# An interleaved HGRN2 and Conformer trunk: VectorE and ScalarE of the first stage in written order, the recurrence's output in the keys' tile, the seam by hand

## The chip, the core and the metric

The kernel runs on one core of a Trainium2 chip. A core has five engines that run their own instruction streams in order: TensorE (PE in the profile) for matrix products, VectorE (DVE), ScalarE (ACT), GpSimd (POOL) and SyncE (SP), which here only issues transfers. They meet through semaphores. An instruction whose semaphore has not come holds up everything behind it on its engine. Products go to PSUM, in eight banks of 128 x 512 floats; everything else lives in SBUF. The metric is the device time of one execution in microseconds (us); lower is better. All values are 32-bit floats.

## The reference, cut to what matters

Two layers over a sequence of 1024 tokens with 1024 channels. The change touches the mixer of the first layer:

```python
def hgrn2_mixer(h, w_in, lb, norm_g, w_out):
    q, fz, v, g = jnp.split(h @ w_in, 4, axis=-1)
    q = silu(q)
    f = lb + (1 - lb) * sigmoid(fz)          # the forget gate
    k = 1 - f
    # per head (8 heads, 128 keys, 128 values), along the tokens:
    #   S_t = diag(f_t) S_{t-1} + k_t v_t^T ,   o_t = S_t^T q_t
    o = recurrence(q, k, v, f)
    o = o * rsqrt(mean(o * o, axis=-1) + RMS_EPS) * norm_g
    return (o * silu(g)) @ w_out
```

What follows (the layer norm, two squared-ReLU networks, a Conformer convolution module as the second mixer, two more layer norms) is the same in both kernels.

## The kernel before

The first stage computes the four projections, the recurrence and the start of the product with w_out. A pair is two blocks of 128 output channels, computed for both halves of the tokens (512 each) with seven products in place of eight (Strassen's scheme, in Winograd's form): `PAIRS` lists twelve pairs, eight of kind q (one head's queries and forget gates) and four of kind g (two heads' output gates), and `ORDER` the seven products, numbered 1, 2, 6, 5, 7, 3, 4. Each product is four quarter products of three matmuls, because each operand is kept as a rounded high part and a low part. `make_form` prepares the weight operand of a product: sums on DVE (tiles pr, total), the high part by a cast on ACT, the low part by a subtraction on DVE (tile fs, in a ring of five). `load_block` fetches the next weight block on SP when a block is used up.

`pair_product` issues a product; after it, its result is taken out of PSUM into a tile t, added to others, and passed through the gate functions by `settled` and `swish` (tiles sq, qk, t). The results of kind q go to the tile qk (queries and keys of one head, 128 x 2048), those of kind g wait in one of four tiles t.

`recurrence(h)` is a generator: each `yield` ends a step. In order: the forget gates F and first scalings; scalings of the queries and keys by products of gates over 1, 2, 4, ... 64 tokens (`scale`, `total`, on DVE, tiles qk and T); between them PE's level products (`levels`), whose results DVE copies under a mask into the tile at (`put`); the transposes of the keys, which ACT copies to the tile kt; the states, a chain of small DVE operations on PE's outer products (`outer`); the outputs (`attend`); the statistics (`settle`: squares on ACT, a scaling on DVE, a power on POOL, copies on ACT to the tile F, called o); and the transposes back (`give`), whose result ACT writes to the tile F again (called on) and SP stores to DRAM (od). Two heads run at a time, the second at least nine steps (`LAG`) behind the first. F, T, kt, kd and at exist once.

`slot()` runs after each quarter product. It counts a tick, which starts jobs that `later` has put off, and by `pace` it lets `step()` take one step of a recurrence. So the order on PE, POOL and SP is the written one, in which the recurrence's steps stand between quarter products. The order on DVE and ACT in this stage is not: after `early_order.close()` a scheduler with a timeline model chooses it. `gate_some` and `gate_out` load a stored head half (u), multiply it with its gate, and store it (zd).

`block_sums` adds weight blocks of the later networks in DRAM: two plain copies of 1 MB on SP, then three accumulating transfers on POOL. Twelve of them fall into this stage.

The last pair overlaps with the loading and splitting of w_out (tiles wb, wa) and of the gated heads (tile back to oT) in `tail`; then the first three output blocks of w_out are computed with seven of eight row blocks each, the last head is finished (`last_head`), and the eighth row block follows.

In the profile most DVE, PE and POOL instructions have line 173, the helper that issues them. They are told apart by their tiles.

Of the kernel before, what the change touches and what calls it, by code (L numbers as in the profile page):

```python
# [15 lines left out]
P = 128  # L16
# [3 lines left out]
H = 8  # L20
# [217 lines left out]
def body(ctx, tc, d, out):  # L238
# [102 lines left out]
    order.enter_context(tc.manual_schedule(engines={mybir.EngineType.PE, mybir.EngineType.Pool, mybir.EngineType.SP}))  # L341
# [106 lines left out]
    early_order = ExitStack()  # L448
    early_order.enter_context(tc.manual_schedule(engines={mybir.EngineType.DVE, mybir.EngineType.Activation}))
# [99 lines left out]
    def make_form():  # L549
# [5 lines left out]
        hi, lo = s[:, 0], s[:, 1]  # L555

        def plus(out, x, y):
            vector.tensor_tensor(out=out, in0=x, in1=y, op=ALU.add)

        if i == 6:  # L560
# [5 lines left out]
        if i == 2:  # L566
            plus(b[0], b[0], b[2])
        made.append(s)
        if i in (5, 7, 3, 4):
            free.append(b[{5: 2, 7: 0, 3: 1, 4: 3}[i]])  # L570
            load_block()
# [16 lines left out]
    def recurrence(h):  # L588
# [3 lines left out]
        F = p1("f")  # L592
        vector.tensor_scalar(out=F, in0=K, scalar1=GATE_EPS, scalar2=None, op0=ALU.max)
        nc.scalar.activation(K, K, AF.Identity, bias=qs, scale=-QSCALE)
        mul(Q, Q, F)
        T = p1("T")
# [15 lines left out]
        def grow(n):  # L612
            total(n)
            scale(n)

        def levels(a, b, n=P):
            for s in range(0, n2, n):
                tensor.matmul(level_ps[:, s // P, :], a[:, s : s + n], b[:, s : s + n], start=True, stop=True)
# [3 lines left out]

        total(1)
        yield
        scale(1)
        yield
        grow(2)
# [9 lines left out]
        scale(4)  # L637
        yield
# [11 lines left out]
        scale(16)  # L650
        total(32)
        yield
        for n in (32, 64):
# [3 lines left out]
            scale(n)  # L657
            if n == 32:
                total(64)
# [9 lines left out]
        nc.scalar.copy(out=kt[:, :nk], in_=level_ps[:, :nk])  # L669
        yield  # L670
        state = None
        o, on = F.rearrange("p (a b) -> p a b", b=P), F

        def settle(half):
            ss = stat.tile([P, 2, 4], F32, tag="ss", name="ss")
            sq = p1("sq")
            for c in range(NTB):
                nc.scalar.activation(sq[:, c * P : (c + 1) * P], out_ps[:, half * NTB + c, :], AF.Square, scale=1.0 / QSCALE, accum_out=ss[:, 0, c : c + 1])
            vector.tensor_scalar(out=ss[:, 1], in0=ss[:, 0], scalar1=1.0 / P, scalar2=RMS_EPS, op0=ALU.mult, op1=ALU.add)
            power_m_half(ss[:, 0], ss[:, 1], 4)  # L680
            for c in range(NTB):
                nc.scalar.activation(o[:, half * NTB + c], out_ps[:, half * NTB + c, :], AF.Copy, scale=ss[:, 0, c : c + 1])

        def give(half):
            part = slice(half * HT, (half + 1) * HT)
            for c in range(half * NTB, half * NTB + NTB):
                tensor.transpose(out_ps[:, c, :], o[:, c], ident)
            nc.scalar.activation(on[:, part], out_ps[:, half * NTB : half * NTB + NTB].rearrange("p a b -> p (a b)"), AF.Copy, scale=nrm[:, h : h + 1])
            if h == H - 1:
# [56 lines left out]
    def settled(kind, j, m, n, t, ps=None):  # L746
        if kind == "g":
            if t is None:
                t = p1("t")
# [887 lines left out]
```

## Time and profile before

| | us |
|---|---|
| median of three runs (lowest, highest) | 2174.51 (2171.23, 2177.52) |
| the profiled execution | 2174.34 |
| its span, on which all positions below are counted | 2172.5 |
| PE, DVE, ACT, POOL busy in it | 2103.5, 1451.1, 1043.4, 369.0 |

The pair products start at 91.3 us and the stage's last waits of PE lie before 504 us. The views used below are: the busy times of the engines, in the whole and in stretches (PE, weight load, DVE, ACT and POOL, then the mean granted clock of PE, the DMA share and GB/s); the list of waits (who waited for whom: total us, times, longest us); the chain that ended last (start, us, what); groups of instructions (busy us and mean ns of one, then the idle time before them); instructions in order of time, with the idle time before them in brackets; and the transfers by their issuing queue (KB, median us from issue to landing). PEld is the weight load of PE, which overlaps its products.

### The profile page before, as it was taken

To read this page: it belongs to the slowest core of one execution; us is meant where nothing else is said; L and a number is where in the kernel's file an instruction comes from. 1 tells how busy PE (TensorE), PEld (TensorE's weight loads), DVE (VectorE), ACT (ScalarE), POOL (GpSimd) and SP (SyncE) were. 2 spreads that over 40 slices of the span, in tenths; PEclk is the share of its full clock that TensorE was granted. 3 is DMA by queue.
4 is the path that set the end of the run, shared out by engine and by line. 5 is a ranking of instruction groups with operands and counts; after the bars stand their busy time and mean duration, and the time that the engine had idled before them with its cause. 6 is when DMAs were issued, how large, how long until landed. Compare 5 with 4: busy or idle time off the path is not lost.

```text
span 2172.5 us, 27149 instructions
## 1 busy us (share of the span) xinstructions
PE 2103.5 (97%) x10056; PEld 1747.4 (80%) x10056; DVE 1451.1 (67%) x1890; ACT 1043.4 (48%) x1599; POOL 369.0 (17%) x344
## 2 busy tenths in 40 slices
PE   8998897899999999999999999999999999999998
PEld 6777786777888888888888888888878888888886
DVE  8596776776777666656666799799727544554446
ACT  5444343343156555644445576558542443443333
POOL 0011111100100000000001499289211000000001
PEclk9999999999999999999999999999999999999999
DMA  4486887755269976899998855664495888866552
GB/s 177 164 228 169 236 210 198 186 141 207 79 192 300 306 277 213 285 387 326 342 332 319 301 193 179 219 241 166 158 312 206 316 323 308 313 203 194 194 165 98
DMA packets 174357, 508.62 MB, mean 234 GB/s; under 512 B 16528, under 2 KB 45456, under 8 KB 173200
## 3 DMA queue, kind: packets, MB, share of 16 engines
q1 hardware_dynamic: 165264, 473.32, 61.3%
q0 software_dynamic: 8960, 33.56, 8.7%
q8 instruction: 79, 1.29, 0.2%
q14 instruction: 54, 0.44, 0.1%
HBM read 377.32 MB, written 196.61 MB: 264 GB/s over the span
## 4 chain that ended last, share of the span: by engine, by line
PE 82%; DMA 6%; DVE 6%; POOL 3%; issue 1%; ACT 1%; SPq 0%; DVEq 0%; POOLq 0%; ACTq 0%
PE ps L173 82%; POOL cb L173 3%; DMA od<-f 2%; DVE qk L173 1%; DMA wa<-ready 1%; DMA raw<-in_w_dram 1%; DMA u<-od 1%; DMA pr<-in_wp_dram 1%; DMA vr<-in_wv_dram 1%; DVE at L173 0%; DVE vr L173 0%; DVE fs L173 0%; DVE xf L173 0%; DVE t L173 0%; ACT xf L390 0%
## 5 line engine op out<-in xcount | busy, mean ns | idle before, releaser
L173 PE MATMUL ps<-dw,dh 128*128 128x512 f32 x2688 | 611.0, 389 | 0.0
L173 PEld LDWEIGHTS ps<-dw,dh 128*128 128x128 f32 x2688 | 504.3, 188 | 104.3
L173 PE MATMUL ps<-x1f,fw 128*128 128x512 f32 x1344 | 307.9, 390 | 0.8 <-DVE c L173 0.8
L173 PEld LDWEIGHTS ps<-x1f,fw 128*128 128x128 f32 x1344 | 251.5, 188 | 52.9 <-issue 1.2
L173 PE MATMUL ps<-xa,wa 128*128 128x512 f32 x1152 | 268.8, 392 | 0.0
L173 PE MATMUL ps<-xf,fs 128*128 128x512 f32 x1008 | 264.2, 413 | 0.0
L173 PEld LDWEIGHTS ps<-xa,wa 128*128 128x128 f32 x1152 | 214.3, 188 | 43.3
L173 POOL TENSOR_TENSOR cb<-cb,prod 128x512 f32<-128x512 f32 x176 | 234.3, 1341 | 17.6 <-ACT prod L1405 7.1
L173 PEld LDWEIGHTS ps<-xf,fs 128*128 128x128 f32 x1008 | 192.3, 198 | 38.6
L173 DVE TENSOR_TENSOR dh<-dh 128x1024 fp32r<-128x1024 f32 x112 | 136.5, 1223 | 114.1 <-ACT dh L70 114.0
L173 DVE TENSOR_TENSOR dw<-dr,dw 128x1024 fp32r<-128x1024 f32 x112 | 136.7, 1223 | 105.3 <-ACT dw L70 104.8
L173 DVE SCALAR_TENSOR_TENSOR ps<-u,par,ps 128x512 f32<-128x512 f32 x288 | 198.7, 750 | 9.9 <-ACT ps L1417 8.5
L70 ACT CAST dh<-dh 128x1024 fp32r<-128x1024 f32 x112 | 117.1, 1050 | 144.9 <-DMA dh<-hf 143.0
L70 ACT CAST dw<-dr 128x1024 fp32r<-128x1024 f32 x112 | 117.4, 1053 | 138.7 <-PE ps L173 126.4
L173 PE MATMUL ps<-xc,wa 128*128 128x512 f32 x768 | 174.4, 389 | 0.0
L173 PEld LDWEIGHTS ps<-xc,wa 128*128 128x128 f32 x768 | 144.1, 188 | 29.8
L475 POOL TENSOR_TENSOR mv<-mv,nhalf 128x1 f32<-128x1 f32 x32 | 46.3, 1447 | 681.3 <-DVE mv L173 681.3
L1405 ACT ACTIVATE prod<-u,par 128x512 f32<-128x512 f32 x176 | 125.3, 722 | 54.1 <-POOL cb L173 53.3
L173 DVE TENSOR_TENSOR wa<-raw,wa 128x1024 fp32r<-128x1024 f32 x55 | 71.4, 1300 | 69.6 <-ACT wa L70 69.5
L70 ACT CAST wa<-raw 128x1024 fp32r<-128x1024 f32 x55 | 57.8, 1050 | 118.4 <-PE ps L173 108.8
L173 PE MATMUL ps<-vw,xf 128*128 128x512 f32 x336 | 82.1, 408 | 9.2 <-ACT vw L390 5.1
L173 PE MATMUL ps<-xb,wa 128*128 128x512 f32 x384 | 89.3, 391 | 0.0
(196 smaller groups left out, 2609.5 us busy)
## 6 DMA issues: line engine op xcount, KB each, us to landing
wa<-ready SPq DMA_DIRECT2D x122, 512.0 KB, 4.6
dh<-hf SPq DMA_DIRECT2D x112, 512.0 KB, 4.8
ready<-spare SPq DMA_DIRECT2D x74, 512.0 KB, 4.8
sum_w<-in_w_dram SPq DMA_DIRECT2D x32, 1024.0 KB, 9.4
dr<-sum_w SPq DMA_DIRECT2D x64, 512.0 KB, 4.4
raw<-in_w_dram SPq DMA_DIRECT2D x51, 512.0 KB, 4.4
dr<-in_w_dram SPq DMA_DIRECT2D x48, 512.0 KB, 4.6
raw<-in_w1q_dram SPq DMA_DIRECT2D x36, 512.0 KB, 4.3
```

The lines of the kernel that those rows point to most:

```text
L70: self.nc.scalar.copy(out=slot[:, 0, c], in_=raw[:, c])
L173: return op(*args, **kw)
L475: nc.gpsimd.tensor_tensor(out=dst, in0=src, in1=nhalf[:, :n], op=ALU.pow)
L1405: nc.scalar.activation(tp, u[:, k : k + HT], AF.Copy, scale=tap(j, k))
```

## The change

1. DVE and ACT follow the written order through the whole first stage. For that the operations that depend on PE or on one another are put off with `later`: a product's result is taken out one quarter product after its end (`evacuate`), a gate's multiplication two after its sigmoid, the low part of a weight form one after the high part, each scaling and masked copy of the recurrence one after the products it follows, the copies after the statistics three after the squares. One form more is made ahead, and a head joins the waiting recurrences four quarter products later.
2. The normalised output is written into kt (`on`), not F; the squares go to F, not to sq; the statistics' scaling runs on POOL, not on DVE.
3. The loads of u, the multiplications with the gates and the stores are paced by ticks (`gate_turn`): a load at least seven ticks after the head's store, the product at least nine after the load, the store two after it. The product is written over the gate, and that tile is stored.
4. The two plain copies of `block_sums` in this stage are issued by POOL.
5. The end of the stage is a list of jobs with ticks (`seam`): loads and splits of w_out and of the heads, two heads to an operation. The first three output blocks are computed together, row block by row block.

```diff
-    order.enter_context(tc.manual_schedule(engines={mybir.EngineType.PE, mybir.EngineType.Pool, mybir.EngineType.SP}))
+    order.enter_context(tc.manual_schedule(engines={getattr(mybir.EngineType, e) for e in ("PE", "Pool", "SP", "DVE", "Activation")}))
...
+        queue = nc.sync if after is not None else nc.gpsimd
...
-        nc.sync.dma_start(out=v[:, 0:2], in_=w[:, 0:4:2])
-        later(gap // 2, lambda: nc.sync.dma_start(out=v[:, 2:4], in_=w[:, 0:2]))
+        queue.dma_start(out=v[:, 0:2], in_=w[:, 0:4:2])
+        later(gap // 2, lambda: queue.dma_start(out=v[:, 2:4], in_=w[:, 0:2]))
...
-        cut(hi, lo, total if i == 6 else b[{1: 0, 2: 1, 5: 2, 7: 0, 3: 1, 4: 3}[i]])
...
+        def low():
+            vector.tensor_tensor(out=lo, in0=raw, in1=hi.bitcast(F32), op=ALU.subtract)
+            if i == 2:
+                plus(b[0], b[0], b[2])
+            if i in (5, 7, 3, 4):
+                free.append(raw)
+                load_block()
+        def high():
+            nc.scalar.copy(out=hi, in_=raw)
+            later(wait, low)
+        later(wait if i in (6, 5) else 0, high)
...
         levels(K, Q)
-        grow(8)
-        put(1)
+        total(16)
+        later(1, lambda: (scale(8), put(1)))
         yield
         levels(kd[:, 1], kd[:, 0])
-        put(0)
-        total(16)
+        total(32)
+        later(1, lambda: put(0))
         yield
...
-        put(2)
         dec = p1("dec")
-        vector.tensor_copy(out=dec, in_=totals[P])
+        later(1, lambda: (scale(64), put(2), vector.tensor_copy(out=dec, in_=totals[P])))
         yield
...
-        o, on = F.rearrange("p (a b) -> p a b", b=P), F
+        o, on = F.rearrange("p (a b) -> p a b", b=P), kt.rearrange("p a b -> p (a b)")
...
-            for c in range(NTB):
-                nc.scalar.activation(sq[:, c * P : (c + 1) * P], out_ps[:, half * NTB + c, :], AF.Square, scale=1.0 / QSCALE, accum_out=ss[:, 0, c : c + 1])
-            vector.tensor_scalar(out=ss[:, 1], in0=ss[:, 0], scalar1=1.0 / P, scalar2=RMS_EPS, op0=ALU.mult, op1=ALU.add)
+            for c in cs:
+                nc.scalar.activation(o[:, c], out_ps[:, c, :], AF.Square, scale=1.0 / QSCALE, accum_out=ss[:, 0, c % NTB : c % NTB + 1])
+            nc.gpsimd.tensor_scalar(out=ss[:, 1], in0=ss[:, 0], scalar1=1.0 / P, scalar2=RMS_EPS, op0=ALU.mult, op1=ALU.add)
             power_m_half(ss[:, 0], ss[:, 1], 4)
+            def rest():
+                for c in cs:
+                    nc.scalar.activation(o[:, c], out_ps[:, c, :], AF.Copy, scale=ss[:, 0, c % NTB : c % NTB + 1])
+                ready.add(half)
+            later(3, rest)
...
         outer(range(NTB))
+        later(1, lambda: chain(range(NTB)))
         yield
         attend(range(NTB))
         outer(range(NTB, nk))
-        settle(0)
+        later(1, lambda: (chain(range(NTB, nk)), settle(0)))
...
+            if k == 3:
+                later(1, lambda: evacuate(p, i, st, ps))
+            slot()
...
+    def gate_turn():
+        now = ticks[0]
+        if to_load and len(loaded) < 2 and done.get(to_load[0], now) <= now - 7:
+            at = to_load.pop(0)
+            u = p1("u")
+            nc.sync.dma_start(out=u, in_=od[at[0]][at[1]])
+            loaded.append((at, u, now))
+        if loaded and loaded[0][0] in gates and loaded[0][2] <= now - 9:
+            (h, half), u, _ = loaded.pop(0)
+            g = gates.pop((h, half))
+            mul(g, u, g)
+            def store():
+                nc.sync.dma_start(out=zd[half][:, h, :], in_=g)
+                stored[h, half] = ticks[0]
+            later(2, store)
...
+    def seam():
+        plan = [
+            (5, lambda: fetch(0, 0)), (15, lambda: split_w(0, 0, 136)), (17, lambda: split_w(0, 1, 144)), (19, lambda: split_w(0, 3, 120)),
+            (21, lambda: split_w(0, 2, 152)), (13, lambda: heads_in(0, 0, 4, 32)), (19, lambda: heads_in(0, 4, 6, 32)),
...
+            (43, lambda: last_in(H - 2, 1, sixth[1])), (46, lambda: last_in(H - 1, 1, lastly[1])),
+        ]
+        for n, job in plan:
+            later(n, job)
...
+    make_form()
+    tick(4)
...
         if kind == "q":
-            recs.append(j)
+            later(4, lambda j=j: recs.append(j))
...
+    for k in range(KB):
+        for (t, n), ps in zip(early_out, (banks[:, i] for i in range(3))):
+            (lh, ll), (rh, rl) = wide(oT[0][0], t, ws[n])[k]
+            tensor.matmul(ps, lh, rh, start=k == 0, stop=False)
+            tensor.matmul(ps, lh, rl, start=False, stop=False)
+            tensor.matmul(ps, ll, rh, start=False, stop=k == KB - 1)
             slot()
```

More of the change, by code (lines that the diff above doesn't have):

```diff
@@ L626, in recurrence @@
         yield
-        grow(2)
+        total(2)
+        scale(2)
         yield
@@ L695, in recurrence @@
[L695 to L697 removed]
+                done[h, half] = ticks[0]
+            later(1, end)
         def values(c):
@@ new lines, in body, with take, silu, evacuate @@
+    recs, active, pace, alone = [], [], [0.0, 0.0], [False]
+    LAG = 9
+    def take():
+        at = owners["at"] % 4
+        owners["at"] += 1
+        assert owners.get(at) not in gates, owners[at]
+        owners[at] = None
+        return p1("t"), at
+    owners = {"at": 0}
+    def silu(out, t, then):
+        sg = p1("sq")
+        nc.scalar.activation(sg, t, AF.Sigmoid)
+        later(2, lambda: (mul(out, t, sg), then()))
+    def evacuate(p, i, st, ps):
+        kind, j = PAIRS[p]
+        m, n = {2: (0, 0), 7: (1, 1), 3: (0, 1)}.get(i, (1, 0))
+        def gate(t, at):
+            def then():
+                gates[2 * j + m, n] = t
+                owners[at] = (2 * j + m, n)
+            return then
+        if i in (1, 6, 5):
+            st[i] = take()
+            nc.scalar.copy(out=st[i][0], in_=ps)
@@ L766, in body @@
+        if kind == "g":
+            later(1, lambda: silu(t, t, gate(t, at)))
+        elif m == 0:
+            later(1, lambda: silu(qk[j][:, 0, part], t, lambda: None))
+        else:
+            later(1, lambda: gated_key(t, 1.0))
     turn_of = {"z": 0, "a": 1, "b": 2}
     def pair_product(p, i, f, st):
-        kind, j = PAIRS[p]
         ps = banks[:, st["banks"]["a" if i == 2 else "b" if i in (5, 3) else "z"]]
```

263 lines of the change are left out of this document (96 added, 167 removed).

## The prediction

> **What bounds the kernel now.** I read the page, then the busy time by stage, the waits of the stage that the change touches, and its chain.
>
> ```profile
> PE 2103.5 (97%) x10056; PEld 1747.4 (80%) x10056; DVE 1451.1 (67%) x1890; ACT 1043.4 (48%) x1599; POOL 369.0 (17%) x344
> PE 82%; DMA 6%; DVE 6%; POOL 3%; issue 1%; ACT 1%; SPq 0%; DVEq 0%; POOLq 0%; ACTq 0%
> ```
> ```profile
> 91.30:504.00 412.70, 365.17 (x2244) 309.04 (x2243) 302.21 (x464) 183.26 (x419) 50.31 (x51) 0.95 0.75 201
> 620.00:1400.00 780.00, 779.17 (x3519) 646.09 (x3518) 550.48 (x695) 440.47 (x608) 167.00 (x171) 1.00 0.80 281
> 1400.00:2172.00 772.00, 761.02 (x3409) 629.16 (x3407) 447.98 (x519) 344.88 (x458) 137.11 (x104) 0.99 0.66 229
> ```
>
> TensorE bounds the whole, and from 620 us on it is idle for 12 us in all. In the 412.7 us of the pair products and the recurrence (the busy times stand in the order PE, weight load, DVE, ACT, POOL, then the clock) it is idle for 412.7 - 365.2 = 47.5 us, and its granted clock is 0.95 on average. DVE is the next busiest, 302 us or 73%. Who holds PE up, and who holds up DVE:
>
> ```profile
> PE ps L173 <- DVE qk L173: 25.7, 11, 6.0
> PE ps L173 <- DVE at L173: 18.2, 7, 5.5
> DVE ss L173 <- ACT sq L678: 16.9, 13, 3.3
> DVE u L173 <- DMA u<-od: 11.8, 6, 5.9
> DVE total L173 <- DMA pr<-in_wp_dram: 9.5, 3, 5.6
> DVE f L173 <- DMA od<-f: 9.2, 4, 4.4
> ```
> ```profile
> 172.70 9.65 DMA od<-f
> ...
> 182.45 0.71 DVE f L173
> ...
> 183.18 1.23 DVE qk L173
> ...
> 188.27 1.80 PE ps L173 x33
> ```
> ```profile
> 188.27 1.07 PE L173 MATMUL ps<-qk 128*32 128x32 f32 x32 [5.95 <-DVE qk L173]
> 227.83 2.46 PE L173 MATMUL ps<-kd 128*128 128x128 f32 x12 [4.36 <-DVE at L173]
> 286.47 1.07 PE L173 MATMUL ps<-qk 128*32 128x32 f32 x32 [3.59 <-DVE qk L173]
> 377.08 3.78 PE L173 MATMUL ps<-qk 128*128 128x128 f32 x16 [5.53 <-DVE at L173]
> ```
>
> Nearly all PE idle time is a level product of the recurrence that waits for DVE's scaling (qk) or its masked copy (at). The chain shows why: a store of the finished head out of tile F lands after 9.65 us, DVE stands at the next head's first write to F, and the older head's scaling is queued behind it. Of the four gaps, 188 and 286 are of this kind; 227 comes after DVE's wait for u, 377 after its wait for weights.
>
> The stops also cost clock:
>
> ```profile
> 138.00:144.00 6.00, 3.61 (x39) 2.98 (x38) 6.00 (x8) 1.56 (x2) 1.12 (x3) 1.00 0.72 171
> 186.00:192.00 6.00, 3.73 (x38) 3.10 (x39) 6.00 (x9) 1.23 (x2) 0.00 (x0) 0.62 0.91 251
> 192.00:198.00 6.00, 6.00 (x34) 4.67 (x33) 6.00 (x8) 1.54 (x3) 0.00 (x0) 0.81 0.00 0
> ```
>
> After 2.4 us of idle (138 to 144) it stays 1.00; after the gap of 5.95 us it is 0.62, and then 0.81 with PE fully busy. At most 0.05 x 365 = 18 us are lost so in the stage; I take 15, since the dips stand where PE works. So 47.5 + 15 = 62.5 us can be had here, no more.
>
> **The change part by part.** (1) The output goes into the keys' tile: the 9.2 us of DVE waits go. The store must now land before the same tile takes the next head's keys. In the written order that write stands more than ten quarter products behind the second store, over 7 us by the row of a product below, with the recurrence's own products between; a landing of 9.65 us, as above, about fits. The squares now go to F as well, which nothing else uses at that time. I count nothing; the bounds are 0 and the 9.65 us, once a head, if every store were late.
>
> (2) DVE and ACT in written order, each operation one to three quarter products behind its source. PE keeps its work; only the recurrence's steps move, by up to four quarter products. The gate load is issued nine quarter products ahead of its product, so the 11.8 us of u go; the 16.9 us of ss move to POOL. What is late next is DVE itself, in arrears where a written stretch asks more of it than PE takes. Rows for this:
>
> ```profile
> L173 DVE TENSOR_TENSOR qk<-qk,T 128x1024 f32<-128x1024 f32 x48 | 58.2, 1219 | 7.6 <-PE ps L173 7.6
> L173 DVE TENSOR_TENSOR fs<-pr,fs 128x512 fp32r<-128x512 f32 x72 | 49.4, 688 | 28.6 <-ACT fs L390 28.5
> L173 DVE COPY_PREDICATED at<-mask,ps 128x1024 f32<-128x1024 int32 x24 | 32.3, 1344 | 1.6 <-PE ps L173 1.6
> L173 DVE TENSOR_TENSOR qk<-qk,f 128x1024 f32<-128x1024 f32 x16 | 19.5, 1222 | 0.2
> ```
> ```profile
> L173 PE MATMUL ps<-xf,fs 128*128 128x512 f32 x77 | 17.6, 389 | 0.0
> ```
> ```profile
> L173 PE MATMUL ps<-xf,fs 128*128 128x512 f32 x61 | 15.4, 399 | 0.0
> L173 PE MATMUL ps<-qk 128*64 128x64 f32 x16 | 1.1, 225 | 0.6 <-DVE qk L173 0.6
> L173 PE MATMUL ps<-qk 128*32 128x32 f32 x32 | 0.7, 197 | 2.4 <-DVE qk L173 2.4
> ```
>
> A quarter product is three matmuls: 17.6/77 x 3 = 0.69 us alone, 15.4/61 x 3 = 0.76 us among recurrence work. I read DVE's list per quarter product off the new program. Worst stretch, head five: nine quarter products, from the release of its scaling over 16 to its key transposes, hold three scalings or products over 1024 and the start of the next head (4 x 1.22), one masked copy (1.34), eleven operations of 128x512 (11 x 0.69) and a small one (0.17): 14.0 us. PE takes 9 x 0.69 + 0.7 + 1.1 = 8.0 us. So PE stands for 5.9 us there in all, spread over three waits. Head two comes to 12.6 - 8.0 = 4.5 us on its keys and 0.9 at its states. The same count gives 5.6, 3.5, 5.4, 2.5, 3.5, 6.1, 2.5 and 4 for the heads in order: 33 us. With 0.76 for a quarter product it is some 5 less. I take 30, against 47.5 now: 17.5 gained. The bounds: 8 (DVE's 302 us lie under 365 of PE, and arrears could be worked off before they matter) and 47.5 (nothing but a change of place).
>
> (3) Clock: two or three of these waits pass 3 us each; by the pair at 186 and 192, (0.38 x 3.73) + (0.19 x 6) = 2.6 us apiece, so 5 to 8 us, against 15. I take 7: 8 gained; bounds 0 and 15. "TensorE: Matmul & The Clock Gate" in the Trainium skill, section Part 1, puts the threshold at an idle window of about 3.4 us; by that only the largest wait would cost clock, some 4 us less would be lost, and the time would be 2148. The trace has no wait between 2.4 and 2.8 us to place it better.
>
> (4) POOL takes the statistics' scaling and 24 plain copies from SP:
>
> ```profile
> sum_w<-in_w_dram SPq DMA_DIRECT2D x24, 1024.0 KB, 8.8
> sum_w<-in_w_dram POOLq DMA_DIRECT2D x12, 1024.0 KB, 12.5
> ```
> ```profile
> L378 POOL DMA_DIRECT2D sum_w<-sum_w x24 | 20.7, 863 | 145.0 <-DMA sum_w<-in_w_dram 100.7 <-DMA sum_w<-sum_w 44.2
> L376 POOL DMA_DIRECT2D sum_w<-in_w_dram x12 | 16.5, 1379 | 38.6 <-DMA sum_w<-in_w_dram 38.5
> L475 POOL TENSOR_TENSOR ss<-ss,nhalf 128x4 f32<-128x4 f32 x16 | 16.4, 1024 | 193.8 <-DVE ss L173 193.8
> ```
>
> 24 issues at 1.38 us and 16 scalings at about 1.02 us are 50 us more for POOL, which waits 194 us for ss now: covered. But ACT now waits in written order for ss: four squares, two POOL operations (2.05 us), with three quarter products (2.1 us) allowed. I price the overshoot at 0 to 1 us for 16 halves, some of it reaching PE: 4 us lost, bounds 0 and 48 (the rival below). On SP the weight loads no longer queue behind those copies; I count nothing for it, bounds 0 and the 9.5 us of total.
>
> (5) The tail by hand:
>
> ```profile
> 473.00:504.00 31.00, 25.09 (x165) 20.44 (x164) 20.99 (x32) 15.49 (x38) 1.03 (x1) 0.89 0.67 214
> ```
>
> Its 5.9 us idle are in the 47.5. The early output blocks go block of rows by block of rows, so the last head is needed at their end; its splits are written some ten quarter products ahead. Behind them the order of PE, DVE and ACT is the same instruction for instruction, so nothing else is counted.
>
> Sum: -17.5 - 8 + 4 = -21.5 us on the profiled execution's 2174.34 us (span 2172.5, 1.8 around it): 2152.8, say 2152. The median of the runs shown is 2174.51, the same for this purpose.
>
> **The rivals.** *DVE keeps up.* Idle 8, clock 2: 52.5 us gained, 2122. For it: DVE is 73% busy and loses 47 us of its own to the four waits listed above. Against: the load is uneven, 14.0 us against 8.0 in the stretch worked out.
>
> *The stalls only change place.* Every reordering leaves DVE's 302 us, and a strict order lets one late cast on ACT hold the level work, as the store did. Idle 44, clock 14: 2170, within 0.3%, which is about what a measurement of this kernel can tell from no change.
>
> *The statistics stand behind POOL's transfers.* POOL waits 183.6 us for its sums now, 5.1 us for each of the 36 accumulating issues; with the copies in the same queue, an ss queued behind such a wait is late by one or two of them, ACT stands at it in written order, and so do the casts that DVE needs. At 6 us a head that is 48 us instead of 4: 2152 + 44 = 2196. It decides from (21.5 + 4)/8 = 3.2 us a head. Against: now POOL reaches most statistics early; in the new order three heads have such a wait right ahead. "DMA: Bandwidth & Descriptors" in the Trainium skill, section SWDGE vs HWDGE vs iDMA, speaks against this move: plain copies belong to SP's or ACT's queue, and GpSimd's to accumulation, because it writes the descriptors itself. No run here shows a plain copy on POOL.
>
> **How the numbers follow.** The forecast, 2152, ranges by its bounds from 2135 to 2167 and has 0.58; DVE keeping up 0.14; a change of place 0.11; POOL's transfers 0.17. Faster: 0.58 + 0.14 = 0.72; same 0.11; slower 0.17. The range, 2118 to 2182, takes in the best rival and stops short of the slower one; it leaves out some 0.2.
>
> **What would show it.** Right: no wait of DVE for the od store or for u, PE idle near 30 us between 91 us and the end of the stage, mostly ahead of key transposes and states, the clock near 0.98, the stage some 20 us shorter, the rest equal. Wrong: ACT waiting for POOL's ss by more than 10 us in all, POOL's waits for its sums ahead of ss, or DVE waiting on ACT's casts in the level steps; and any difference after the first stage.

## The result, and the profile after

The changed kernel takes 2125.95 us in the median (2124.27 to 2126.95, four runs), the kernel before, beside it on the same chip, 2173.61 (2171.23 to 2177.52): a ratio of 0.978, 95% interval 0.976 to 0.980. That is 48 us less; the forecast had 21.5. The gain is more than twice the one worked out. The time lies inside the range given only because a rival's end of it reaches that far; the forecast's own bounds were 2135 to 2167.

The profiled execution's span is 2123.9 us. The engines' line and the chain's shares, from the page of the changed kernel:

```profile
PE 2088.5 (98%) x10056; PEld 1736.5 (82%) x10056; DVE 1448.7 (68%) x1868; ACT 1036.6 (49%) x1593; POOL 393.7 (19%) x384
PE 84%; DVE 5%; DMA 5%; POOL 3%; ACT 2%; issue 1%; SPq 0%; DVEq 0%; POOLq 0%
```

TensorE still bounds the whole; its instructions are as many, and their busy time fell by 15.0 us. Where the time went is seen in the place of the first output product, the first thing behind the stage. From the timelines of PE, the kernel before and then the changed one:

```profile
504.06 6.40 PE L173 MATMUL ps<-wb,oT 128*128 128x512 f32 x27
```
```profile
455.26 2.89 PE L173 MATMUL ps<-w,oT 128*128 128x512 f32 x12
```

From there to the end it is 2172.5 - 504.1 = 1668.4 us before and 2123.9 - 455.3 = 1668.6 after. All of the gain, 48.8 us of span, lies ahead of that point. Inside the stage, busy time by stretches in the changed kernel (start:end and length, then PE, weight load, DVE, ACT, POOL, the granted clock, DMA share, GB/s):

```profile
91.30:455.20 363.90, 349.39 (x2242) 297.95 (x2241) 298.76 (x443) 176.55 (x411) 73.00 (x87) 0.99 0.84 226
473.00:504.00 31.00, 31.00 (x146) 25.87 (x145) 24.23 (x38) 2.15 (x4) 4.90 (x4) 1.00 0.21 75
```

PE's idle time in the stage is 363.9 - 349.4 = 14.5 us, where it was 47.5; and the same products took it 349.4 us instead of 365.2, since the clock is higher. So 33 us come from waits and 16 from PE's shorter busy time, which is the clock. The waits of the changed kernel in that stretch (engine, what it was about to do, who released it: total, times, longest):

```profile
PE ps L173 <- DVE dec L173: 8.9, 5, 3.4
PE ps L173 <- DVE qk L173: 4.2, 2, 3.0
PE ps L173 <- DVE at L173: 1.4, 1, 1.4
```
```profile
DVE fs L173 <- ACT fs L576: 28.0, 21, 6.9
DVE qk L173 <- PE ps L173: 17.9, 19, 2.2
DVE t L173 <- PE ps L173: 7.8, 11, 1.2
...
ACT f L689 <- POOL ss L474: 8.4, 9, 1.6
```

VectorE's waits for the output's store, for u, for late weight blocks and for the squares are gone. Of the 28.0 us that it still waits for ScalarE's casts, 14.7 lie ahead of the first level products, and behind them no wait is longer than 1.6. What is left of PE's waits is nearly all ahead of the key transposes (`dec` is the last small copy that VectorE makes before them) and ahead of the first 128x128 products of two heads; there is none at the 128x32 products, where most of them stood before.

The clock falls in three stretches of 6 us in the stage, and nowhere else in it:

```profile
132.00:138.00 6.00, 5.35 (x25) 4.84 (x26) 4.96 (x8) 1.40 (x2) 1.20 (x1) 0.72 0.83 158
234.00:240.00 6.00, 4.33 (x16) 3.73 (x17) 6.00 (x10) 2.34 (x4) 0.00 (x0) 0.72 1.01 206
360.00:366.00 6.00, 4.03 (x14) 3.47 (x15) 6.00 (x10) 2.64 (x5) 0.61 (x1) 0.72 1.05 313
```

### The profile page after: what moved, and what is told of

It is laid out like the page before. It is cut to its first block, busy times and chain, and to the rows that moved or that the text cites. A ratio compares the mean times of both kernels' runs of the same rounds, so it can differ in the third digit from the quotient of the medians.

```text
span 2123.9 us, 27054 instructions
## 1 busy us (share of the span) xinstructions
PE 2088.5 (98%) x10056; PEld 1736.5 (82%) x10056; DVE 1448.7 (68%) x1868; ACT 1036.6 (49%) x1593; POOL 393.7 (19%) x384
## 4 chain that ended last, share of the span: by engine, by line
PE 84%; DVE 5%; DMA 5%; POOL 3%; ACT 2%; issue 1%; SPq 0%; DVEq 0%; POOLq 0%
PE ps L173 84%; POOL cb L173 2%; DMA raw<-in_w_dram 1%; DVE qk L173 1%; DMA wa<-ready 1%; DMA y<-kept 1%; DMA dh<-hf 1%; DMA vr<-in_wv_dram 1%; DVE vr L173 0%; DVE t L173 0%; DVE fs L173 0%; DVE wa L173 0%; DVE xf L173 0%; DVE at L173 0%; ACT xf L391 0%
## 5 line engine op out<-in xcount | busy, mean ns | idle before, releaser
L173 PEld LDWEIGHTS ps<-dw,dh 128*128 128x128 f32 x2688 | 504.1, 188 | 105.1 <-ACT dh L70 0.7
L173 PE MATMUL ps<-xf,fs 128*128 128x512 f32 x1008 | 254.5, 402 | 0.0
L173 PEld LDWEIGHTS ps<-xf,fs 128*128 128x128 f32 x1008 | 185.6, 191 | 36.3
L173 DVE TENSOR_TENSOR wa<-raw,wa 128x1024 fp32r<-128x1024 f32 x51 | 66.5, 1306 | 65.7 <-ACT wa L70 65.6
L1294 POOL COPY next<-ss 128x1 f32<-128x1 f32 x37 | 17.2, 465 | 407.2 <-DVE spare L173 257.3
```

Of the source, the lines that this page charges most:

```text
L173: return op(*args, **kw)
L1294: nc.gpsimd.tensor_copy(out=raw[:, :1], in_=now)
```

## The experiments

Three questions: which edits carry the 48 us; whether VectorE's arrears are what is left; and what takes the arrears away. Names that begin with `a_` are edits of the changed kernel, with `b_` of the kernel before. Ratios are to the kernel before, which ran beside each.

### Tile and copies, put in or taken out alone

`b_tile` gives the kernel before the output in the keys' tile, `a_on_f` takes that out of the changed kernel, `a_copies_sp` puts the plain copies back on SP:

```diff
# b_tile (a_on_f is the reverse, in the changed kernel)
-        o, on = F.rearrange("p (a b) -> p a b", b=P), F
+        o, on = F.rearrange("p (a b) -> p a b", b=P), kt.rearrange("p a b -> p (a b)")
# a_copies_sp
-        queue = nc.sync if after is not None else nc.gpsimd
+        queue = nc.sync
```

> The kernel before, with one line changed: the normalised output goes to the keys' tile. Theory A (the gain of the change comes from several removed waits together, the store out of F being one): DVE's 9.2 us of waits for the od store go, and with them the PE gaps of 5.95, 3.59 and 3.1 us and their clock, so 10 to 17 us less than before, 2157 to 2164. Rival B (the tile alone carries the gain): 35 us less or more, under 2139. Rival C (the waits only move to the next transfer): within 6 us of before.

> The changed kernel, with the output back in F. Theory A: DVE waits at F again, but the written order leaves some nine quarter products between the second store and the next write to F, so only the slow stores are felt: 3 to 10 us over the changed kernel, 2129 to 2136. Rival B: over 20 us, 2146 or more.

> The changed kernel, with the plain copies of the weight sums back on SP. Theory A (nothing was counted for them): from 3 us less to 6 us more than the changed kernel's 2126. Rival D (the weight loads come sooner because the copies left SP's queue, and that is where the unforeseen 26 us came from): 10 to 25 us more, with DVE waiting for the weight blocks again.

Measured: `b_tile` 2171.1 us, ratio 0.9999 (0.9986 to 1.0012); `a_on_f` 2125.6 and `a_copies_sp` 2126.3, both 0.980 (0.978 to 0.982), as the changed kernel itself. Neither edit is worth anything that the runs can tell, in either kernel: the waits of `b_tile` only changed place (rival C), `a_copies_sp` is as theory A has it, and `a_on_f` is better than both its theories. VectorE waits for the store once in it, 0.9 us, so in the changed kernel the waits for the store are gone without the tile too. In `b_tile` the waits for the store are gone, and PE waits elsewhere: the 5.95 us at 188 us are down to 1.5, but where the kernel before had 3.13 and 3.16 us ahead of key transposes, the timeline of PE now has

```profile
334.88 1.75 PE L173 MATMUL ps<-ident,qk 128*128 128x128 f32 x7 [4.73 <-DVE at L173]
392.26 1.75 PE L173 MATMUL ps<-ident,qk 128*128 128x128 f32 x7 [6.16 <-DVE T L173]
```

### The written order, and its lag

`a_sched` leaves VectorE and ScalarE to the scheduler again from the end of the early part on, and keeps everything else of the change. `a_no_lag` keeps the written order and drops the quarter product of lag in the recurrence and the evacuations; `a_evac0` drops it in the evacuations alone; `a_rec_old` has the old body of the recurrence up to the copy of the transposed keys, in its old order and without lag; the lags of the states and the squares stay.

```diff
# a_sched
-    order.enter_context(tc.manual_schedule(engines={... ("PE", "Pool", "SP", "DVE", "Activation")}))
+    order.enter_context(tc.manual_schedule(engines={... PE, Pool, SP}))
# a_evac0, four places; a_no_lag, eleven more in the recurrence
-                later(1, lambda: evacuate(p, i, st, ps))
+                later(0, lambda: evacuate(p, i, st, ps))
# a_rec_old, one step of several
-        total(16)
-        later(1, lambda: (scale(8), put(1)))
+        total(8)
+        scale(8)
+        put(1)
```

> The changed kernel, with DVE and ACT ordered by the scheduler after the early part, as in the kernel before; tiles, pacing and seam stay changed. Theory A (the written order with its lags is a large part): 2140 to 2165, with PE idle 25 to 40 us in the stage. Rival E (removing the slow waits was all, the order of DVE and ACT does not matter): within 6 us of 2126.

> The changed kernel with the written order kept, and the operations of the recurrence and of the evacuations written right behind their source instead of one quarter product later (fifteen places). Theory L (the written order pays only because each operation stands behind its source's time): an operation that is written at its source heads its engine's queue while PE still works on that source, some 1.2 us of a quarter product, and what stands behind it waits too; VectorE has about 88 such operations and is busy 299 us of 364, so its idle time of 66 us grows by 20 to 60 us, and the time rises by 10 to 45 us, to 2136-2171. Theory R (the order pays, the lag does not): within 5 us of 2126.

> The changed kernel with the body of the recurrence as before the change: no lag, and each product of the decays (T) behind the masked copy and the scaling of the step ahead of it, instead of in front of them. Theory L: as with the lag alone, and the two ops in the new order have a step less in which to be late, so the time is at or above that of the kernel without lag, 2134-2171, and the waits ahead of the 128x32 products and of the key transposes come back (14.5 us in the changed kernel, 40 before). Theory R (order inside the recurrence is worth nothing; the gain is in the evacuations, the gating and the tail): within 5 us of 2126.

> The changed kernel with the evacuations of the quarter products and the two operations behind them written at their source instead of one quarter product later; the recurrence keeps its lag. The kernel without any lag took 15 us more, the one with the old recurrence and no lag in it 1.5 more. Theory E (the 15 us are the evacuations'): 2136-2146. Theory N (they are the recurrence's own, in its new order without a lag): 2122-2130.

Measured: `a_sched` 2143.8 us, 0.988 (0.986 to 0.990); `a_no_lag` 2141.2, 0.985 (0.983 to 0.987); `a_evac0` 2140.3, 0.983 (0.981 to 0.986); `a_rec_old` 2127.5, 0.979 (0.976 to 0.981). So the written order is worth some 18 us of the 48 by the times, 23 by the ratios. Its lag is worth some 14 (12 by the ratio), and the evacuations, with the gate functions behind them, have nearly all of it: dropping the recurrence's lag as well costs 0.9 us more (`a_no_lag`), the old body without lag 1.5 (`a_rec_old`), and neither is clear of the runs' spread. The recurrence's new order without its lag, with the evacuations' lag kept, was not run. Of the two theories on `a_rec_old`, the one I held (the recurrence needs it) falls. PE idles 23.6 us in the stage of `a_evac0`, against 14.5. VectorE waits longer for casts there,

```profile
DVE fs L173 <- ACT fs L576: 38.7, 26, 6.9
```

38.7 us against 28.0. It is not ScalarE's copy of a bank that PE still fills which holds the casts up: its waits are 43.2 us in `a_evac0` and 47.8 in the changed kernel, up to 456 us. What waits longer are the gate functions. Written at their source, they stand ahead of a cast in ScalarE's order and wait for VectorE's sum t, 95.9 us in all (73.5 and 22.4) against 77.8 (63.0 and 14.8). One such place in the timeline of `a_evac0`:

```profile
126.05 0.63 ACT L793 ACTIVATE qk<-t 128x512 f32<-128x512 f32 x1 [4.04 <-DVE t L173]
...
127.44 0.60 ACT L576 CAST fs<-pr 128x512 fp32r<-128x512 f32 x1
...
128.08 0.69 DVE L173 TENSOR_TENSOR fs<-pr,fs 128x512 fp32r<-128x512 f32 x1 [2.06 <-ACT fs L576]
```

### Edits of the change, put into the kernel before

`b_gate` has the paced gating (load, product into the gate's tile, store, each some quarter products behind the other, none forced), `b_rec` the recurrence's order and lags, `b_evac` the evacuations one quarter product later, `b_ahead` one weight part made further ahead. `b_four` has the first three and the tile together. `b_seven` adds `b_ahead`'s edit, the statistics on POOL with their lag, and the output's store two quarter products behind its copy. VectorE and ScalarE stay with the scheduler in all of them.

```diff
# b_gate
-            if i == 5:
-                gate_some(True)
...
     def slot():
         tick()
+        gate_turn()
# b_evac
+            if k == 3:
+                later(1, lambda: evacuate(p, i, st, ps))
# b_ahead
+    make_form()
     for p, (kind, j) in enumerate(PAIRS):
# b_seven, beside b_four and b_ahead
-            vector.tensor_scalar(out=ss[:, 1], in0=ss[:, 0], ...)
+            nc.gpsimd.tensor_scalar(out=ss[:, 1], in0=ss[:, 0], ...)
...
+            later(3, rest)
...
+                    later(2, store)
```

> The kernel before, with VectorE and ScalarE left to the scheduler, and the recurrence written as in the changed kernel (products of the decays first, scalings and masked copies one quarter product later). Theory S (of the 28 us that the change gives without a written order on those two engines, the recurrence's order has the most, since the scheduler goes by the order of emission): 2148-2162. Rival: within 4 us of 2172, as the recurrence's order was worth 1.5 us in the changed kernel.

> The kernel before, with the gating of the heads' outputs paced as in the changed kernel: the load seven quarter products behind the store, the product nine behind the load, into the gate's tile, one store two behind it, none forced at the fifth block. Theory G (forced gating puts several products and transfers in one place, where VectorE's arrears then arise): 2145-2163. Rival C (as with the output's tile alone, the waits only change place): within 5 us of 2172.

> The kernel before, with one more of the weight blocks' parts (a copy on ScalarE, a difference on VectorE, the sums) made ahead of the first stage's loop, so that each is ready one product of twelve matmuls times four, some 5 us and more, earlier than before. Theory F (that distance is what the scheduler lacked: the parts then never press on the recurrence): 2140-2160. Rival: within 5 us of 2173, as PE did not wait for a part of the weights before the change, and the waits only change place.

> The kernel before, with the evacuations of the quarter products emitted one quarter product later. In the changed kernel that lag was worth 14 us, with VectorE and ScalarE in written order. Theory E (it is worth that with the scheduler too): 2155-2165. Rival (the lag is needed only where the order is kept as written; a scheduler finds the place by itself): within 5 us of 2173.

> The kernel before, with four edits of the change that gave nothing alone or are tried here alone, together: output in the keys' tile, paced gating, the recurrence's order, the evacuations one quarter product later; VectorE and ScalarE stay with the scheduler, the weight parts and the tail as before. Theory T (each takes one of several waits that are in series, so that only together they show): 2142-2160. Rival: within 6 us of 2173, and the gain lies in what is not among the four: the parts made further ahead, the statistics' and the output's lags, the tail.

> The kernel before with seven edits of the change: the four of the run with four, and the statistics' scaling on POOL with the square roots' users three quarter products behind, the output's store two behind its copy, one weight part made further ahead; VectorE and ScalarE stay with the scheduler, the tail and the plain copies as before. Theory T (many small waits in series: each engine that is freed of one goes on to the next): 14.0 us of waits for statistics and 19.5 for late blocks go, and it comes near the changed kernel under the scheduler (2143.8) but for the tail: 2142-2152. Rival: no better than four edits, 2158-2165, and the gain lies in the tail or the copies.

Measured, as ratios to the kernel before:

| kernel | us | ratio | interval | PE idle in the stage |
|---|---|---|---|---|
| b_rec | 2174.7 | 1.0003 | 0.9990 to 1.0016 | 50.7 |
| b_gate | 2174.1 | 0.9997 | 0.9983 to 1.0012 | 47.1 |
| b_tile | 2171.1 | 0.9999 | 0.9986 to 1.0012 | 47.1 |
| b_evac | 2169.6 | 0.9994 | 0.9982 to 1.0005 | 47.6 |
| b_ahead | 2168.6 | 0.9984 | 0.9973 to 0.9994 | 47.1 |
| b_four | 2161.5 | 0.9960 | 0.9941 to 0.9980 | 44.6 |
| b_seven | 2151.5 | 0.9891 | 0.9876 to 0.9906 | 33.7 |
| a_sched | 2143.8 | 0.9882 | 0.9864 to 0.9901 | 26.6 |
| changed | 2126.0 | 0.9778 | 0.9761 to 0.9795 | 14.5 |

The last column is length less PE's busy time in the profiled execution, from 91.3 us to the first output product; the kernel before has 47.5. The five single edits give 0.2% in sum, 5 us, and only one of them is outside its own uncertainty. The four that `b_four` joins give 0.07% alone, 1.5 us, and 0.4% together, 9 us (`b_four` is just short of its theory's range); the intervals hardly keep these two apart. Seven give 1.1%, 24 us, as theory T has it and nearly what the change gives without the written order (1.2%). That the waits are in series is seen in the single edits: `b_tile` loses its 9.2 us of waits for the store and `b_gate` its 11.8 us for u, and PE idles as long as before, since an engine that no longer waits for one late thing comes sooner to the next. VectorE's waits in `b_four` show which were next:

```profile
DVE fs L173 <- ACT fs L390: 25.4, 18, 9.5
DVE t L173 <- PE ps L173: 14.4, 10, 3.9
DVE ss L173 <- ACT sq L677: 14.0, 11, 3.3
DVE total L173 <- DMA pr<-in_wp_dram: 12.5, 5, 5.4
DVE state L173 <- PE ps L173: 9.1, 6, 2.5
DVE pr L173 <- DMA pr<-in_wp_dram: 7.0, 2, 5.1
```

The store and u are gone from it, but late weight blocks cost 12.5 + 7.0 = 19.5 us where they cost 9.5 before. In `b_seven` the statistics are gone too, and the blocks' lateness is down to

```profile
DVE total L173 <- DMA pr<-in_wp_dram: 2.3, 2, 2.0
```

Of the three edits that `b_seven` adds, which one does how much was not told apart. Two of them, the statistics on POOL and the later store, were not run alone, so it is not shown that they give nothing alone.

### What is left: VectorE's arrears

`a_more` does the clamp of 128x1024 at each head's start five times. `a_pool_sums` moves two of the five sums of weight blocks to POOL. `a_slide` puts one more step ahead of the key transposes and joins two early ones. `a_front` and `a_front2` write the next head's first operations behind the last scaling and masked copy of the head before; in `a_front` ScalarE's constant scaling of the keys came behind the first scaling by decays instead of ahead of it, so it computes something else, and it is `a_front2` that does only what was meant.

```diff
# a_more
+        for _ in range(5):
             vector.tensor_scalar(out=F, in0=K, scalar1=GATE_EPS, scalar2=None, op0=ALU.max)
# a_pool_sums
-                plus(b[0], b[0], b[2])
+                nc.gpsimd.tensor_tensor(out=b[0], in0=b[0], in1=b[2], op=ALU.add)
+                nc.gpsimd.tensor_tensor(out=b[2], in0=b[2], in1=b[3], op=ALU.add)
# a_slide
         scale(1)
-        yield
         total(2)
...
         yield
+        yield
         nk = 2 * NTB - 1
# a_front2
-        mul(Q, Q, F)
-        total(1)
+        first = [lambda: (mul(Q, Q, F), total(1))]
+        later(4, lambda: first and first.pop()())
```

> The changed kernel with the first operation of each head (the clamp of 128x1024, 0.70 us) done five times instead of once: 4 x 0.61 = 2.4 us more on VectorE at the start of each of eight heads. Theory A (PE's last 14.5 us of waits are VectorE's arrears, and arrears carry over): each head is late by 2.4 us less what VectorE idles on the way (66 us in 364, so some 2 us in a head's stretch of 12), so six to eight heads grow by 0.5 to 2.4 us: 4 to 19 us, to 2130-2145. Theory B (a chain of latencies in the last steps sets the waits; the earlier load does not): 0 to 3 us.

> The changed kernel with two of the five sums of weight blocks per pair moved from VectorE to POOL (24 of 128x512). Theory A (arrears): 24 x 0.61 = 14.6 us less on VectorE in 364; the waits fall by 3 to 8 of 14.5 us and the clock gives 0 to 5 more: 2113-2124. Rival P: POOL takes its instructions in written order and is held 126.9 us by the transfers that sum weights and 114.3 us by ScalarE's squares; VectorE's next sum reads what POOL left, so VectorE, ScalarE's copies and the statistics inherit those waits: slower by 5 to 40 us, 2131-2166.

> The changed kernel with the key transposes one step later in each head: an empty step ahead of them, and the head's second and third step made one, so that the number of steps stays. Theory A (what is left of PE's waits is the work that stands on VectorE ahead of the transposes, longer than the quarter products that PE has in the same stretch): with two to four quarter products more in that stretch, 2.5 us and more, the 10.3 us of waits at the transposes go and 0 to 5 us of clock with them: 2111-2120. Rival M (a wait taken away here comes back in the steps that are now closer together, or behind the transposes that are now later): within 4 us of 2126.

> The changed kernel with the first three VectorE operations of each head (clamp, product, first product of decays: 0.61 + 1.14 + 0.60 = 2.35 us) written up to four quarter products later, behind the last scaling and masked copy of the head before. 2.4 us more at that place cost 33 us. Theory A: the waits at the key transposes (10.3 us, 0.9 to 3.4 each) fall by up to 2.35 each, by 6 to 9 us in all, and the clock gives 0 to 5 more: 2112-2120. Rival M: the next head's own first products of 128x128 wait instead (4.2 us now): within 4 us of 2126.

> The changed kernel with two of a head's first operations on VectorE (the product with the decays, 1.14 us, and the first product of decays, 0.60) written up to four quarter products later, behind the last scaling and masked copy of the head before; the clamp and ScalarE's scaling of the keys stay where they are. Theory A: the six waits at the key transposes (0.89, 2.26, 1.41, 3.36, 1.41, 0.96) fall by up to 1.74 each, to 0.5 and 1.6 and nothing, 8 us in all, and the clock gives 0 to 5 us more: 2113-2120. Rival M (the next head's own chain is then the later one): within 4 us of 2126.

Measured: `a_more` 2158.9 us, 0.994 (0.992 to 0.996), 33 us slower than the changed kernel; `a_pool_sums` 2125.1, 0.978 (0.975 to 0.980); `a_slide` 2129.8, 0.979 (0.976 to 0.981); `a_front` 2150.5, 0.991 (0.989 to 0.992); `a_front2` 2125.0, 0.977 (0.975 to 0.979).

`a_more` is beyond both theories. The groups of PE's instructions by form, up to 490 us, have the key transposes of the changed kernel and then of `a_more` as

```profile
L173 PE MATMUL ps<-ident,qk 128*128 128x128 f32 x56 | 8.9, 307 | 10.3 <-DVE dec L173 8.9 <-DVE at L173 1.4
```
```profile
L173 PE MATMUL ps<-ident,qk 128*128 128x128 f32 x56 | 11.2, 361 | 30.2 <-DVE dec L173 30.2
```

Eight waits instead of six, and 19.9 us more in them: head by head in PE's timelines, seven grow by 2.7 to 2.9 us, and that of the last head, behind which no other starts, does not grow. Five clamps in a row take 3.63 us, 0.73 each, so four more are 2.9 us a head: they reach PE one for one. I had allowed for VectorE's idle time to swallow a part; but the next head's start is written right ahead of the transposes, and in that stretch VectorE has next to none. The stage in `a_more` ends at 489.0 us:

```profile
91.30:489.00 397.70, 358.29 (x2241) 302.64 (x2241) 320.98 (x475) 176.40 (x411) 74.15 (x87) 0.96 0.76 207
```

PE idles 397.7 - 358.3 = 39.4 us in it, against 14.5, so 5 us of the 33 are other waits, and its busy time is 9 us longer, which is clock.

`a_pool_sums` shows the other side. VectorE has 24 operations less, some 14.6 us, and the time is the same (0.8 us less); theory A falls. The waits at the transposes are 8.9 us instead of 10.3. The stage of the profiled execution ends 4.4 us sooner, 3 of them with less clock lost, but behind the stage 3.3 us are lost again, by clock and by waits in the later stages. What is taken away elsewhere does not count; in heads two and five, where one of the moved sums stood in the last stretch, the wait fell by 0.6 and 0.7 us, one operation's time. No engine waits for POOL's sums, so rival P falls as well.

`a_slide` and `a_front2` do take the waits at the transposes away, and get them back. PE's waits in the stage, `a_slide` and then `a_front2`:

```profile
PE ps L173 <- DVE state L173: 6.6, 5, 2.0
PE ps L173 <- DVE at L173: 5.7, 4, 1.7
PE ps L173 <- ACT kt L672: 3.6, 3, 2.1
PE ps L173 <- DVE qk L173: 2.1, 2, 1.4
```
```profile
PE ps L173 <- DVE qk L173: 6.6, 2, 3.8
PE ps L173 <- DVE at L173: 2.2, 2, 1.4
PE ps L173 <- DVE state L173: 1.4, 3, 0.5
PE ps L173 <- DVE dec L173: 1.4, 2, 1.0
PE ps L173 <- ACT kt L674: 1.3, 2, 0.6
PE ps L173 <- ACT f L691: 0.4, 1, 0.4
```

18.0 and 13.3 us in all, against 14.5. The 25 us that `a_front` loses are of another kind: ScalarE's scaling of the keys waits 46.6 us for VectorE in it, the copy to kt stands behind it, and PE waits 18.3 us for that copy. Rival M was right in `a_slide` and `a_front2`, and `a_front2` is no faster than the changed kernel by more than the runs can tell. No version tried here beats it clearly.

## Why the prediction was right about the cause and wrong about the size

The mechanism was the one forecast: DVE's waits for the store, for u and for the squares go, what is left is VectorE's arrears, 10.3 of 14.5 us of them ahead of the key transposes, the tail stands still no longer, and nothing changes behind the stage. The signs given with a number failed: PE's idle time was to be near 30 us, the clock near 0.98 and the stage 20 us shorter, and they are 14.5, 0.99 and 49; and there is no wait left at the states. The sum was -17.5 - 8 + 4 = -21.5; measured it is -33 - 16 + 0 = -49 on the profiled executions. **The step that failed is (2), the arrears: 30 us taken, 14.5 found**; term (3) followed it, and (4) was a loss that did not come.

**(2) The arrears.** Heads zero to seven were counted at 5.6, 3.5, 5.4, 2.5, 3.5, 6.1, 2.5 and 4 us; PE's waits in the timeline are 3.9, 1.2, 2.3, 1.4, 0, 3.4, 1.4 and 1.0. Head five is among the worst in both rows, and every head is counted 1.1 to 3.5 us too high. Head five's stretch, counted at 14.0 us of DVE for 8.0 of PE, shows why. Its VectorE rows in the timeline of the changed kernel, first and last of sixteen with some between, and PE's:

```profile
349.56 1.23 DVE L173 TENSOR_TENSOR qk<-qk,T 128x1024 f32<-128x1024 f32 x1 [0.57 <-PE ps L173]
350.70 0.69 DVE L173 TENSOR_TENSOR t<-u,t 128x512 f32<-128x512 f32 x1
351.30 0.68 DVE L173 TENSOR_TENSOR t<-t,ps 128x512 f32<-128x512 f32 x1
...
359.47 1.22 DVE L173 TENSOR_TENSOR qk<-qk,T 128x1024 f32<-128x1024 f32 x1
360.61 1.31 DVE L173 COPY_PREDICATED at<-mask,ps 128x1024 f32<-128x1024 int32 x1
361.79 0.18 DVE L173 COPY dec<-T 128x8 f32<-128x8 f32 x1
361.86 0.71 DVE L173 SCALAR_TENSOR_TENSOR t<-ps,sq 128x512 f32<-128x512 f32 x1
361.97 1.55 PE L173 MATMUL ps<-ident,qk 128*128 128x128 f32 x7 [3.36 <-DVE dec L173]
```

An operation of 128x512 has 0.69 us and the next one starts 0.60 us behind it; 1.23 is 1.14, and the masked copy's 1.31 is 1.18. The sixteen durations add up to 13.4 us, and they took 361.86 - 349.56 = 12.3. The mean durations from the groups were some 0.1 us too long to be added up. "Perfetto Trace Analysis" in the Trainium skill, section Per-engine timelines, says that a VectorE row ends at the write's acknowledgement, while the next instruction can begin fetching earlier; the trace agrees, with 0.08 to 0.13 us between the next row's start and the end of such a row. One more operation of 128x512 had been counted than stood there. On the other side PE had 12.4 - 3.36 = 9.0 us of work, not 8.0: a quarter product among recurrence work takes 0.76 us, the value that the prediction names and sets aside, and the stretch holds nearly ten of them, not nine. 12.4 - 9.0 is the 3.4 measured; 14.0 - 8.0 was forecast. Head two comes out in the same way, with 11.2 us for the 12.6 counted and 9.0 of PE for 8.0; the other heads were not taken apart. A wait that is a difference of two long sums takes the errors of both.

**Why arrears did not take the place of all waits.** That was the other half of (2), and it was not weighed: an edit alone gives nothing, as `b_tile`, `b_gate`, `b_rec` and `b_evac` show, and the prediction's rival "the stalls only change place" is what each of them does: PE idles 47 to 51 us in all four. It falls for the whole change. That it does because so many waits go at once is how I read `b_four` and `b_seven`; with two edits not run alone it is not proved.

**(3) The clock.** 15 us were taken as lost before, and 7 as left. Over the stage's stretches of 6 us the shortfall of the granted clock adds up to 22.2 us before and 5.0 after. The prediction allowed at most 18, from a mean of 0.95 over busy time, and two stretches worked out by hand; the sum over all stretches is the better way, and the 16 us gained lie just outside the term's bounds (0 and 15). It goes in portions: three stretches of 0.72 after are 3 x 0.28 x 6 = 5.0, 1.7 us each; the 22.2 us before are 13.0 such portions, the 10.2 of `a_sched` are 6.0, the 15.3 of `a_more` are 9.0. "TensorE: Matmul & The Clock Gate" in the Trainium skill, section Part 1, has the gate look at free-running windows of 3413 ns with half clock after an idle one: by that, as an estimate, one idle window costs half of 3.41, which is 1.7, and the trace agrees with that. It does not bear out my use of the page as a threshold for a single wait: in the changed kernel a wait of 2.26 us cost a portion (the stretch from 234 us, above), and before one of 2.39 us cost none (the stretch from 138 us, in the prediction). The two waits in the timelines of PE, before and then after:

```profile
143.75 0.70 PE L173 MATMUL ps<-qk 128*32 128x32 f32 x32 [2.39 <-DVE qk L173]
```
```profile
235.67 1.53 PE L173 MATMUL ps<-ident,qk 128*128 128x128 f32 x7 [2.26 <-DVE dec L173]
```

In `a_sched` two waits of 3.02 us, at 229 and at 360 us, cost two portions and one. The prediction also says that the kernel before has no wait between 2.4 and 2.8 us; it has one of 2.64, at 389 us, and a portion is lost behind it.

**(4) POOL.** ScalarE waits 8.4 us for the statistics, nine times and at most 1.6; over sixteen halves that is 0.5 each, inside the 0 to 1 priced. But none of it reaches PE, so the 4 us were lost nowhere. The rival of 44 us more falls with it. The plain copies cost nothing on POOL's queue and nothing on SP's (`a_copies_sp`). "DMA: Bandwidth & Descriptors" in the Trainium skill, section SWDGE vs HWDGE vs iDMA, would keep such copies off GpSimd's queue; no run here shows a difference in time.

**(1) and (5).** The tile was counted at nothing, and is worth nothing; the waits for the store, which the prediction has go by the tile, are gone with the output in F as well (`a_on_f`). The tail's 5.9 us of idle time were in the budget; all but the 0.96 at the last head's transposes went, and its lost clock (0.89 before). How much of that the edit of the tail has was not run by itself: `a_sched` has that edit and idles 6.1 us between 440 and 472 us, so it is not that edit alone.

Of the rivals, "DVE keeps up" (2122) came nearest in time, 4 us off, and with its 8 us of idle time and 2 of clock it is nearer to the measured 14.5 and 5.0 together than the forecast's 30 and 7. Its cause holds by half: VectorE is still in arrears in seven of eight heads, as forecast, but by less.

## What to carry to other kernels

When several late things hold one in-order engine in turn, removing one can show nothing; try the edits together before dropping any, and look in the trace for what has become next. To price arrears, add start-to-start distances from a saturated stretch rather than mean durations, and count only what is written ahead of the operation that the other engine waits for: 2.9 us put there cost their full length and clock on top, 14.6 us taken away elsewhere gave nothing that the runs can tell. In a written order, put each operation that waits for another engine's result a little behind that result, so that it does not hold up what stands behind it: for the evacuations and the gate functions that was worth some 14 us here. With the scheduler the evacuations' lag alone gave nothing (`b_evac`), but neither did most single edits, so this does not show that a scheduler has no use for it.

## What had not been expected of the hardware

The clock is lost in equal portions of 1.7 us, 13 of them before and 3 after in this stage, so that a third of the gain (16 of 49 us) is clock; and whether a wait of 2.3 to 2.4 us costs one depends on more than its length. In the kernel before, two portions at the end of the stage, from 492 us on, follow waits of 1.35 us and less. These counts are of one execution each: over the runs of the kernel before the mean granted clock is 0.983 to 0.991, so the number of portions is not the same each time. VectorE's rows overlap: sixteen operations in a row took 12.3 us where their durations add up to 13.4.
